# A 1024 x 1024 x 4096 feed-forward product by seven block products in place of eight, and the two feed-forward products one after the other

## The chip, the cores and the metric

The kernel runs on one core of one Trainium2 chip. The metric is the device time of one execution in microseconds: before the change 1409.34 us, the median of three runs (1408.54 to 1409.73). TensorE multiplies matrices and writes PSUM; VectorE, ScalarE and GpSimd do the element-wise work; SyncE issues the DMAs between DRAM and SBUF.

## The reference, cut to what matters

One layer of a hybrid decoder, 1024 tokens, d_model 1024, d_ff 4096, all float32. The change touches only its last lines, and what feeds them:

```
x = x + g1 * (mixed @ w_out[i])
h2 = rms_norm(x, norm2_g[i]) * (1.0 + sc2) + sh2
ff = jnp.square(jax.nn.relu(h2 @ w_ff1[i])) @ w_ff2[i]      # (1024x1024)(1024x4096), then (1024x4096)(4096x1024)
x = x + g2 * ff
```

## The kernel before

Float32 accuracy is made of reduced-precision products. Every operand is split into a high and a low part of type fp32r (`split`, L457: the high part is a rounding copy, the low part a subtraction, L468), and `mm3` (L87 to L91) gives three matmuls for each product: high x high (L89), high x low (L90), low x high (L91). Below, FF1 is `h2 @ w_ff1` with its squared relu, and FF2 the product with `w_ff2`.

`outproj` (L1464) goes over eight blocks of 128 tokens. `proj(t)` is the output projection of a block (48 matmuls into `pS`), then the gated residual and the norm on VectorE (`xn`, L1483 to L1490). `modulate(t)` transposes `xn` on TensorE, scales and shifts it (`h`, L1502 and L1503) and splits it: high parts `h2h` on ScalarE, low parts `h2l` on GpSimd. `h2h` and `h2l` hold the whole of h2, transposed, 128 x 8 x 1024. The products of the first two 128-wide column chunks of `w_ff1` are begun here, in pieces of 512, 384 and 128 tokens, so that the last block's norm is covered.

`ff` (L1535) interleaves the two products. `ff1(c)` computes one of 32 chunks of 128 columns: 48 matmuls of 512 tokens into a pair of PSUM banks (`pS`), relu and square on ScalarE (`ftr`, `ah`), square again and low part on VectorE (`al`, L1590, L1591). The activations never leave SBUF. `ff2(g)` uses two chunks at once: 16 tiles of 128 tokens x 512 columns, six matmuls each, in four rotating banks (`pg`), each added by VectorE into `acc` (L1607, L1609). The weights come by DMA as whole 512 KB chunks (`fraw`) and are split on ScalarE (`w1h`, `w2h`) and GpSimd (`w1l`, `w2l`). FF1 has 32 x 48 = 1536 matmuls of 512 columns, FF2 16 x 96 = 1536. `ada_g2` computes the gate of the last residual on the side, with one-column matmuls (L265).

The tile framework puts the instructions in order on each engine by a simulated timeline; each engine then works strictly in its own order and waits on semaphores.

## Time and profile before

| | us |
|---|---|
| median of three runs | 1409.34 |
| profiled execution | 1406.54 |
| its span | 1404.5 |
| TensorE busy | 1293.0 |
| VectorE busy | 801.2 |
| GpSimd busy | 545.4 |
| ScalarE busy | 516.1 |
| TensorE idle between 684.8 and 1404 us | 4.6 |

The two feed-forward products fill the second half of the span. Busy time of a row is what the profiler attributes to the instructions; for TensorE, matmuls overlap in the pipeline, so their durations are longer than the distance from one start to the next, and the cadence is read from a stretch divided by its count. Of the 4.6 us of idle time (0.54 and 4.07 us in two stretches) the trace puts 1.2 us down to waits for other engines.

### The profile page before, as it was taken

To read this page: it belongs to the slowest core of one execution; us is meant where nothing else is said; L and a number is where in the kernel's file an instruction comes from. 1 tells how busy PE (TensorE), PEld (TensorE's weight loads), DVE (VectorE), ACT (ScalarE), POOL (GpSimd) and SP (SyncE) were. 2 spreads that over 40 slices of the span, in tenths; PEclk is the share of its full clock that TensorE was granted. 3 is DMA by queue.
4 is the path that set the end of the run, shared out by engine and by line. 5 is a ranking of instruction groups with operands and counts; after the bars stand their busy time and mean duration, and the time that the engine had idled before them with its cause. 6 is when DMAs were issued, how large, how long until landed. Compare 5 with 4: busy or idle time off the path is not lost.

```text
span 1404.5 us, 18004 instructions
## 1 busy us (share of the span) xinstructions
PE 1293.0 (92%) x6822; PEld 1107.2 (79%) x6822; DVE 801.2 (57%) x1422; ACT 516.1 (37%) x954; POOL 545.4 (39%) x425
## 2 busy tenths in 40 slices
PE   4978988818898999999999999999999999999998
...
GB/s 334 112 47 39 70 104 124 80 132 25 82 86 98 222 153 87 100 90 108 91 150 105 46 40 36 60 51 55 31 60 60 45 110 72 60 60 45 36 25 119
DMA packets 101656, 121.06 MB, mean 86 GB/s; under 512 B 25408, under 2 KB 75584, under 8 KB 101568
## 3 DMA queue, kind: packets, MB, share of 16 engines
...
q10 hardware_dynamic: 1072, 0.03, 0.0%
...
## 4 chain that ended last, share of the span: by engine, by line
PE 59%; DMA 4%; DVE 2%; ACT 2%; POOL 1%; issue 1%; SPq 0%; ACTq 0%; POOLq 0%; DVEq 0%
PE pS L90 10%; PE pS L89 10%; PE pS L91 10%; PE pg L89 8%; PE pg L91 8%; PE pg L90 8%; DMA awa<-w_ada 3%; PE po L1270 1%; PE pg L265 1%; PE pg L1254 1%; POOL wol L468 1%; DMA woraw<-w_out 1%; ACT P L1243 0%; PE pg L1458 0%; DVE aacc L1401 0%
## 5 line engine op out<-in xcount | busy, mean ns | idle before, releaser
L1609 DVE TENSOR_TENSOR acc<-pg,acc 128x512 f32<-128x512 f32 x240 | 164.5, 689 | 243.0 <-PE pg L91 242.8
L468 POOL TENSOR_TENSOR w2l<-fraw,w2h 128x1024 fp32r<-128x1024 f32 x32 | 78.9, 2488 | 328.4 <-ACT w2h L466 328.4
L90 PE MATMUL pg<-w2l,ah 128*128 128x512 f32 x512 | 201.0, 393 | 0.0
L89 PE MATMUL pg<-w2h,ah 128*128 128x512 f32 x512 | 200.5, 392 | 0.6 <-DVE acc L1607 0.5
L91 PE MATMUL pg<-w2h,al 128*128 128x512 f32 x512 | 200.6, 393 | 0.2 <-DVE al L1591 0.2
L90 PE MATMUL pS<-h2l,w1h 128*128 128x512 f32 (+2 forms) x504 | 198.0, 393 | 0.0
L89 PE MATMUL pS<-h2h,w1h 128*128 128x512 f32 (+2 forms) x504 | 196.9, 391 | 0.0
L91 PE MATMUL pS<-h2h,w1l 128*128 128x512 f32 (+2 forms) x504 | 196.7, 390 | 0.0
L466 ACT ACTIVATE w2h<-fraw 128x1024 fp32r<-128x1024 f32 x32 | 32.2, 1052 | 352.5 <-PE pg L91 352.5
L1590 DVE TENSOR_TENSOR ftr<-ftr 128x1024 f32<-128x1024 f32 x32 | 46.2, 1445 | 129.2 <-ACT ah L1589 129.1
L468 POOL TENSOR_TENSOR w1l<-fraw,w1h 128x1024 fp32r<-128x1024 f32 x30 | 74.1, 2470 | 112.3 <-ACT w1h L466 66.2
L89 PEld LDWEIGHTS pg<-w2h,ah 128*128 128x128 f32 x512 | 96.6, 189 | 23.8 <-DVE acc L1607 1.1
L90 PEld LDWEIGHTS pg<-w2l,ah 128*128 128x128 f32 x512 | 96.6, 189 | 21.9
L91 PEld LDWEIGHTS pg<-w2h,al 128*128 128x128 f32 x512 | 96.3, 188 | 21.8 <-DVE al L1591 0.9
L89 PEld LDWEIGHTS pS<-h2h,w1h 128*128 128x128 f32 x504 | 94.6, 188 | 21.6
L91 PEld LDWEIGHTS pS<-h2h,w1l 128*128 128x128 f32 x504 | 94.6, 188 | 21.0
L90 PEld LDWEIGHTS pS<-h2l,w1h 128*128 128x128 f32 x504 | 94.6, 188 | 20.7
L90 PE MATMUL pg<-wl,hh 128*128 128x256 f32 (+1 forms) x288 | 82.1, 286 | 11.4 <-POOL wl L468 11.4
L466 ACT ACTIVATE w1h<-fraw 128x1024 fp32r<-128x1024 f32 x30 | 31.8, 1060 | 160.9 <-PE pS L90 96.2
L89 PE MATMUL pg<-wh,hh 128*128 128x256 f32 (+1 forms) x288 | 81.4, 286 | 3.6 <-ACT wh L466 2.6
L91 PE MATMUL pg<-wh,hl 128*128 128x256 f32 (+1 forms) x288 | 81.9, 285 | 0.0
L1270 PE MATMUL po<-v,pt 128*128 128x64 f32 x576 | 77.8, 283 | 3.5 <-ACT pt L1257 3.4
...
## 6 DMA issues: line engine op xcount, KB each, us to landing
fraw<-w_ff SPq DMA_DIRECT2D x62, 512.0 KB, 3.8
awa<-w_ada SPq DMA_DIRECT2D x32, 512.0 KB, 4.6
x<-x SPq DMA_DIRECT2D x16, 512.0 KB, 5.1
wa<-w_ada SPq DMA_DIRECT2D x13, 512.0 KB, 7.8
...
x_d<-x SPq DMA_DIRECT2D x8, 512.0 KB, 2.6
```

What stands on the lines that cost most here:

```text
L89: T.matmul(out, lh, rh, start=start, stop=False)
L90: T.matmul(out, lh, rl, start=False, stop=False)
L91: self.pe = T.matmul(out, ll, rh, start=False, stop=stop).ins
L265: nc.tensor.matmul(ps[:, k:k + 1], acc.rearrange("p (q k) -> p k q", k=8)[:, k, :], self.ones[:, 0:1], start=True, stop=True)
L466: nc.scalar.activation(hi, x, AF.Copy)
L468: e.tensor_tensor(lo, x, f(hi), op=OP.subtract)
L1254: T.transpose(ps[:, o:o + 128], P[n][h][:, (k0 + i) * 128:(k0 + i + 1) * 128], self.ident)
L1270: T.matmul(po[:, o:o + HD], pt[:, (2 * i + h) * 128:(2 * i + h + 1) * 128], self.v[:, k0 + i, kv * HD:(kv + 1) * HD], start=(o == 0 and k0 ...
L1590: V.tensor_tensor(tr, tr, tr, op=OP.mult)
L1609: V.tensor_tensor(d, ps, d, op=OP.add)
```

## The change

Each pair of 128-wide chunks of `w_ff1` (16 pairs, 256 columns) is one 2 x 2 block product: blocks of the weights 512 x 128, blocks of h2 512 x 512 (`self.B`: half of the features by half of the tokens). The seven-product form by Winograd is used. With B11 = `b00`, B21 = `b10`, B22 = `b11`, and H0, H1 the two feature halves of the last 512 tokens, T1 = H0 - B11 (made in `modulate`, kept as `b01`), T2 = H1 - T1 (in four score slots, `sx`, tags sc4 to sc7), T3 = T2 - B11 and T4 = B21 - T2 are operands; of the weights four sums are made for each pair (`wsum`). A product is 4 x 3 matmuls, a pair 7 x 12 = 84, where two chunks had 96. PSUM accumulates across products where one is a term of two answers: `keep` copies a bank aside in between, into the slots sc4, sc5 and sc6. `put` adds, applies relu, squares, and the finished activations go to DRAM as float32 (`a_d`, 512 KB twice for each pair). When all pairs are done `ff_down` begins: it loads them back (`araw`), splits them (`ah` on ScalarE, `al` on VectorE), loads and splits `w_ff2` as before, and runs FF2 unchanged. In `split` the sums and the T operands have their low parts on VectorE ("v"), and the sums themselves are made on GpSimd.

```diff
             h2p, h2p_close = self.pool("h2", side="left")
-            self.h2h = h2p.tile([128, KC, L], F32R, name="h2h")
-            self.h2l = h2p.tile([128, KC, L], F32R, name="h2l")
+            self.B = {(kk, hf): [h2p.tile([128, 4, 512], F32R, name=f"b{kk}{hf}{n}") for n in "hl"]
+                      for kk, hf in ((0, 0), (0, 1), (1, 0), (1, 1))}
             self.w1p, w1_close = self.pool("w1", side="left")
-            self.w1first = tuple(self.w1p.tile([128, KC, 128], F32R, name=n) for n in ("w1h", "w1l"))
+            self.gb = gb
             self.outproj(mxp)
             mx_close()
             wop_close()
-            self.ff()
+            self.ff_up()
             w1_close()
+            h2p_close()
+            self.ff_down()
             gb_close()
-            h2p_close()
             scp_close()
...
                 bc = lambda w: w[:, 4 * kk:4 * kk + 4, None].to_broadcast([128, 4, 128])
                 V.tensor_tensor(h, pv, bc(self.s2), op=OP.mult)
                 V.tensor_tensor(h, h, bc(self.b2), op=OP.add)
-                hv = self.h2h[:, 4 * kk:4 * kk + 4, t * 128:(t + 1) * 128]
-                self.split(hv, self.h2l[:, 4 * kk:4 * kk + 4, t * 128:(t + 1) * 128], h, "s", "g")
-
-        def loadw1(c, hi, lo):
+                if hf and kk == 0:
+                    for b in self.B[0, 0]:
+                        V.tensor_tensor(h, h, f(b[:, :, tl]), op=OP.subtract)
+                bh, bl = self.B[kk, hf]
+                self.split(bh[:, :, tl], bl[:, :, tl], h, "s", "g")
+                H.append(h)
+            if hf:
+                self.t2[t - 4] = self.sct(t)
+                V.tensor_tensor(self.t2[t - 4], H[1], H[0], op=OP.subtract)
...
+                self.split(*A[i], raw[:, 4 * i:4 * i + 4], "s", "g")
+
+        self.t2 = {}
...
+            if t >= 5 and t < 7:
+                self.W1[t - 5] = self.w1ab(t - 5)
+                loadw1(2 * (t - 5), self.W1[t - 5])
+        self.ff_ps = {i: self.bank2() for i in range(2)}
+        for i in range(2):
+            self.prod(self.ff_ps[i][:, 0], self.W1[i][0], self.B[0, 0], True)
+            self.prod(self.ff_ps[i][:, 1], self.W1[i][1], self.B[1, 0], True)
+            if i == 0:
                 modulate(NT - 1)
...
+    def sct(self, i, dt=F32, n="sx"):
+
+        t = self.scp.tile([128, max(512, (i + 1) * 128)], dt, name=f"{n}{i}", tag=f"sc{i}")
+        return t[:, :512].rearrange("p (k n) -> p k n", k=4)
+
+    def w1ab(self, i):
+
+        if i % 2:
+            w = [self.sct(j, F32R, "w1x") for j in range(4)]
+        else:
+            w = [self.w1p.tile([128, 4, 128], F32R, name=f"w1a{j}") for j in range(4)]
+        return [w[0:2], w[2:4]]
+
+    def prod(self, o, A, B, start):
+        for k in range(4):
+            self.mm3(o, A[0][:, k], A[1][:, k], B[0][:, k], B[1][:, k], start and k == 0, k == 3, skip_group_check=True)
+
+    def ff_up(self):
+
         nc, a = self.nc, self.a
...
-        fp, fclose = self.pool("ff", side="right")
+        fp, fclose = self.pool("ffu", side="right")
+        NP2 = DFF // 256
+        w1 = a["w_ff1"][0].rearrange("(p k) f -> p k f", k=8)
+        self.a_d = self.dram.tile([DFF // 128, 128, 1024], F32, name="a_d")
+        TT = {n: [fp.tile([128, 4, 512], F32R, name=f"t{n}{x}") for x in "hl"] for n in (2, 3, 4)}
+        B11, T1, B21, B22 = (self.B[q] for q in ((0, 0), (0, 1), (1, 0), (1, 1)))
+        RAW, SUM, W, PS, C = {}, {}, {}, {}, {}
+
+        def load(i):
+            RAW[i] = fp.tile([128, KC, 256], F32, name="w1r", bufs=2)
+            D.dma_start(RAW[i], w1[:, :, i * 256:(i + 1) * 256])
+
+        def quarter(i, r, c):
+            return RAW[i][:, 4 * c:4 * c + 4, r * 128:(r + 1) * 128]
+
+        def wsum(i, n):
+            q = lambda r, c: quarter(i, r, c)
+            x, y, op = {1: lambda: (q(1, 0), q(1, 1), OP.add), 2: lambda: (SUM[i, 1], q(0, 0), OP.subtract),
+                        3: lambda: (q(0, 0), q(1, 0), OP.subtract),
+                        4: lambda: (q(0, 1), SUM[i, 2], OP.subtract)}[n]()
+            SUM[i, n] = fp.tile([128, 4, 128], F32, name="ws", bufs=4)
+            G.tensor_tensor(SUM[i, n], x, y, op=op)
+
+        def form(i, n):
+            if n in ("a", "b"):
+                if i not in self.W1:
+                    self.W1[i] = self.w1ab(i)
+                x, w = quarter(i, 0, "ab".index(n)), self.W1[i]["ab".index(n)]
+            else:
+                x = quarter(i, 1, 1) if n == "d" else SUM[i, n]
+                w = [fp.tile([128, 4, 128], F32R, name="wf", bufs=14) for _ in range(2)]
+            self.split(*w, x, "s", "v")
+            W[i, n] = w
+
+        def tform(n):
+            for t in range(4):
+                tl = slice(128 * t, 128 * t + 128)
+                x = self.t2[t]
+                if n > 2:
+                    x = fp.tile([128, 4, 128], F32, name="ws", bufs=4)
+                    b = [f(z[:, :, tl]) for z in (B11 if n == 3 else B21)]
+                    if n == 3:
+                        G.tensor_tensor(x, self.t2[t], b[0], op=OP.subtract)
+                        G.tensor_tensor(x, x, b[1], op=OP.subtract)
+                    else:
+                        G.tensor_tensor(x, b[0], self.t2[t], op=OP.subtract)
+                        G.tensor_tensor(x, x, b[1], op=OP.add)
+                self.split(TT[n][0][:, :, tl], TT[n][1][:, :, tl], x, "s", "v")
+
+        def half(i, r):
+            if (i, r) not in C:
+                C[i, r] = self.gb.tile([128, 1024], F32, name="c0", tag="g1") if r == 0 else \
+                    self.scp.tile([128, 1024], F32, name="c1", tag="sc7")
+            return C[i, r]
+
+        def put(i, r, c, x, y):
+            o = half(i, r)[:, 512 * c:512 * c + 512]
+            if y is not None:
+                V.tensor_tensor(o, x, y, op=OP.add)
+                x = o
+            else:
+                S.activation(o, x, AF.Relu)
+            V.scalar_tensor_tensor(o, x, 0.0, o, op0=OP.max, op1=OP.mult)
+
+        def keep(i, j, x):
+            o = self.sct(j, n="kp").rearrange("p k n -> p (k n)")
+            S.activation(o, x, AF.Copy)
+            C[i, "k", j] = o
+
+        def step(i, n):
+            if i not in PS:
+                PS[i] = [self.ff_ps[i] if i in self.ff_ps else self.bank2(), None]
+            pa, pb = PS[i][0][:, 0], PS[i][0][:, 1]
+            if n == 1:
+                if i not in self.ff_ps:
+                    self.prod(pa, W[i, "a"], B11, True)
+                keep(i, 4, pa)
+            elif n == 2:
+                if i not in self.ff_ps:
+                    self.prod(pb, W[i, "b"], B21, True)
+                put(i, 0, 0, pb, C.pop((i, "k", 4)))
+            elif n == 5:
+                PS[i][1] = self.bank()
+                self.prod(PS[i][1], W[i, 1], T1, True)
+                keep(i, 6, PS[i][1])
+            elif n == 6:
+                self.prod(pa, W[i, 2], TT[2], False)
+                keep(i, 5, pa)
+            elif n == 7:
+                self.prod(pa, W[i, 3], TT[3], False)
+                put(i, 1, 1, pa, C.pop((i, "k", 6)))
+            elif n == 3:
+                self.prod(PS[i][1], W[i, 4], B22, False)
+                put(i, 0, 1, PS[i][1], C.pop((i, "k", 5)))
+                D.dma_start(self.a_d[2 * i], half(i, 0))
+            elif n == 4:
+                self.prod(pa, W[i, "d"], TT[4], False)
+                put(i, 1, 0, pa, None)
+                D.dma_start(self.a_d[2 * i + 1], half(i, 1))
+
+        ORDER = ((1, "a", ()), (5, 1, (1,)), (6, 2, (2,)), (2, "b", ()), (7, 3, (3,)), (3, 4, (4,)), (4, "d", ()))
+
+        def prep(i, j):
+            if i < NP2:
+                _, w, sums = ORDER[j]
+                for n in sums:
+                    wsum(i, n)
+                form(i, w)
+
+        for i in range(2):
+            load(i)
+        for i in range(2):
+            wsum(i, 1)
+            form(i, 1)
+            wsum(i, 2)
+        tform(2)
+        for i in range(2):
+            form(i, 2)
+        tform(3)
+        for i in range(2):
+            wsum(i, 3)
+            form(i, 3)
+        for i in range(2):
+            wsum(i, 4)
+            form(i, 4)
+        tform(4)
+        for i in range(2):
+            form(i, "d")
+            load(i + 2)
+        for i in range(2):
+            step(i, 1)
+            step(i, 5)
+            step(i, 6)
+            step(i, 2)
+            step(i, 7)
+            step(i, 3)
+            step(i, 4)
+            for j in range(7):
+                if i == 1:
+                    prep(2, j)
+        for i in range(2, NP2):
+            for j, (n, _, _) in enumerate(ORDER):
+                step(i, n)
+                prep(i + 1, j)
+            if i + 2 < NP2:
+                load(i + 2)
+        fclose()
...
+    def ff_down(self):
+        nc, a = self.nc, self.a
+        V, S, G, T, D = nc.vector, nc.scalar, nc.gpsimd, nc.tensor, nc.sync
+        fp, fclose = self.pool("ffd", side="left")
...
+        def loada(c):
+            raw = fp.tile([128, 1024], F32, name="araw", bufs=2)
+            D.dma_start(raw, self.a_d[c])
+            ah = fp.tile([128, 1024], F32R, name="ah", bufs=4)
+            al = fp.tile([128, 1024], F32R, name="al", bufs=4)
+            self.split(ah, al, raw, "s", "v")
             aT[c] = ah, al
+
+        for c in range(GF):
+            load2(c)
+            loada(c)
+        acc = fp.tile([128, NT, 1024], F32, name="acc")
...
         for g in range(n):
-            if g + 1 < n:
-                ff1(2 * g + 2)
-            if g + 2 < n:
-                load1(2 * g + 4)
+            for c in range(2 * g + 2, min(2 * g + 4, NF)):
+                load2(c)
+                loada(c)
             if 0 < g < 7:
                 next(ada, None)
                 next(ada, None)
             if g == 7:
                 D.dma_start(self.g2, self.g_d[1:2, :].to_broadcast([128, 1024]))
             ff2(g, g == n - 1)
-            if g + 1 < n:
-                load2(2 * g + 2)
-                load2(2 * g + 3)
-                ff1(2 * g + 3)
-            if g + 2 < n:
-                load1(2 * g + 5)
         fclose()
```

GpSimd, from the end of the normalisation of the last token block into FF1. Before (`h2l` is the low half of a block, `w1l` and `w2l` low parts of whole weight chunks):

```order
L468 TENSOR_TENSOR h2l<-h_7655,h2h 128x4x128
L468 TENSOR_TENSOR h2l<-h_7665,h2h 128x4x128
L468 TENSOR_TENSOR w1l<-fraw,w1h 128x1024
L468 TENSOR_TENSOR w2l<-fraw,w2h 128x1024 x2
L468 TENSOR_TENSOR w1l<-fraw,w1h 128x1024 x2
L468 TENSOR_TENSOR w2l<-fraw,w2h 128x1024 x2
```

After, the same place (`b01l`, `b11l` are the last block's low halves; L1586 is `wsum`, L1607 and L1608 make T3, L1610 begins T4; two rows like the first and second here stand between them and the last `b01l`):

```order
L1586 TENSOR_TENSOR ws<-w1r 128x512
L1586 TENSOR_TENSOR ws<-ws,w1r 128x512
L1607 TENSOR_TENSOR ws<-sx_7394,b00h 128x512
L1607 TENSOR_TENSOR ws<-sx_7524,b00h 128x512
L1608 TENSOR_TENSOR ws<-ws,b00l 128x512 x2
L1607 TENSOR_TENSOR ws<-sx_7620,b00h 128x512
L1607 TENSOR_TENSOR ws<-sx_7670,b00h 128x512
L1608 TENSOR_TENSOR ws<-ws,b00l 128x512 x2
L1586 TENSOR_TENSOR ws<-w1r 128x512 x2
L1586 TENSOR_TENSOR ws<-w1r,ws 128x512 x2
L1610 TENSOR_TENSOR ws<-b10h,sx_7394 128x512
```

From the last low half on, GpSimd has seventeen operations of 128 x 512 up to the first that reads `sx_7394` for T4, the first of the four T2 slots; before, it had weight splits here.

ScalarE, the same place. Before:

```order
L466 ACTIVATE h2h<-h_7655 128x4x128
L466 ACTIVATE h2h<-h_7665 128x4x128
L466 ACTIVATE w1h<-fraw 128x1024
L1586 ACTIVATE ftr<-pS 128x1024
L466 ACTIVATE w2h<-fraw 128x1024
L1589 ACTIVATE ah<-ftr 128x1024
L466 ACTIVATE w2h<-fraw 128x1024
L1586 ACTIVATE ftr<-pS 128x1024
```

After (`t2h` and `t3h` are high parts of T operands, `wf` of weight operands, `kp` is a copy made by `keep`):

```order
L467 ACTIVATE t2h<-sx_7394 128x4x128
L467 ACTIVATE t2h<-sx_7524 128x4x128
L467 ACTIVATE t2h<-sx_7620 128x4x128
L467 ACTIVATE t2h<-sx_7670 128x4x128
L467 ACTIVATE wf<-ws 128x512 x4
L467 ACTIVATE t3h<-ws 128x4x128 x4
L467 ACTIVATE wf<-ws 128x512 x4
L467 ACTIVATE wf<-w1r 128x512
L1631 ACTIVATE kp_7821<-pS 128x512
L1631 ACTIVATE kp_7836<-pg 128x512
```

The first copy out of a product's bank stands behind four high parts of T3 and the high parts of all eight weight sums of the first two pairs, each of which reads a result of GpSimd.

VectorE, in the middle of FF2. Before (`ftr` and `al` are the square and the low part that FF1's chunks need):

```order
L1609 TENSOR_TENSOR acc<-pg,acc 128x512 x13
L1590 TENSOR_TENSOR ftr<-ftr 128x1024
L1591 TENSOR_TENSOR al<-ftr,ah 128x1024
L1609 TENSOR_TENSOR acc<-pg,acc 128x512 x2
L1590 TENSOR_TENSOR ftr<-ftr 128x1024
L1609 TENSOR_TENSOR acc<-pg,acc 128x512
L1591 TENSOR_TENSOR al<-ftr,ah 128x1024
L1609 TENSOR_TENSOR acc<-pg,acc 128x512 x13
```

After:

```order
L1761 TENSOR_TENSOR acc<-pg,acc 128x512 x15
L469 TENSOR_TENSOR al<-araw,ah 128x1024
L1761 TENSOR_TENSOR acc<-pg,acc 128x512
L469 TENSOR_TENSOR al<-araw,ah 128x1024
L1761 TENSOR_TENSOR acc<-pg,acc 128x512 x15
```

In a group of sixteen accumulations VectorE now has two low parts with one accumulation between them; before it had two squares and two low parts, at two places of the group.

## Rows read from the trace of the kernel before

**Rows 1.** The page: span, busy time by engine, chain by engine.
```profile
span 1404.5 us, 18004 instructions
...
PE 1293.0 (92%) x6822; PEld 1107.2 (79%) x6822; DVE 801.2 (57%) x1422; ACT 516.1 (37%) x954; POOL 545.4 (39%) x425
...
PE 59%; DMA 4%; DVE 2%; ACT 2%; POOL 1%; issue 1%; SPq 0%; ACTq 0%; POOLq 0%; DVEq 0%
```

**Rows 2.** Busy time by stretch; columns: us, each engine's busy us (instructions), clock, DMA.
```profile
684.80:722.00 37.20, 36.66 (x203) 32.17 (x203) 23.23 (x19) 11.51 (x14) 16.85 (x9) 1.00 0.42 132
722.00:1404.00 682.00, 677.93 (x2932) 551.38 (x2930) 281.91 (x339) 119.33 (x118) 178.45 (x72) 1.00 0.19 61
```

**Rows 3.** The same view, TensorE alone, inside the two interleaved products.
```profile
1000.00:1300.00 300.00, 300.00 (x1302) 1.00 0.20 60
```

**Rows 4.** Timeline, TensorE, second product alone: start, us, what; 22 rows from first to last.
```profile
1395.51 0.39 PE L91 MATMUL pg<-w2h,al 128*128 128x512 f32 x1
...
1400.27 0.39 PE L91 MATMUL pg<-w2h,al 128*128 128x512 f32 x1
```

**Rows 5.** What TensorE waited for from 640 us on: us in total, times, longest.
```profile
PE pS L89 <- DVE xn L1483: 0.5, 1, 0.5
PE pg L89 <- DVE acc L1607: 0.5, 1, 0.5
PE pg L91 <- DVE al L1591: 0.2, 1, 0.2
```

**Rows 6.** Timeline, TensorE, end of the last output projection.
```profile
684.61 0.40 PE L91 MATMUL pS<-woh,ml 128*128 128x512 f32 x1
684.85 1.05 PE L1498 MATMUL pg<-ident,xn 128*128 128x128 f32 x8
```

**Rows 7.** Timeline, VectorE, while the last token blocks are normalised.
```profile
642.47 1.21 DVE L1484 TENSOR_TENSOR x<-xn,x 128x1024 f32<-128x1024 f32 x1
643.60 1.79 DVE L1503 TENSOR_TENSOR h<-h,b 128x512 f32<-128x512 f32 x1
...
687.82 0.68 DVE L1503 TENSOR_TENSOR h<-h,b 128x512 f32<-128x512 f32 x1
...
692.14 1.79 DVE L1490 TENSOR_SCALAR xn<-x,ors 128x1024 f32<-128x1024 f32 x1 [0.73 <-POOL ors L85]
```

**Rows 8.** Timeline, GpSimd, the same stretch.
```profile
642.69 2.15 POOL L468 TENSOR_TENSOR h2l<-h,h2h 128x512 fp32r<-128x512 f32 x1 [6.79 <-ACT h2h L466]
...
666.33 2.51 POOL L468 TENSOR_TENSOR w1x<-w1r,w1x 128x512 fp32r<-128x512 f32 x2 [3.26 <-ACT w1x L466]
...
699.19 2.92 POOL L468 TENSOR_TENSOR h2l<-h,h2h 128x512 fp32r<-128x512 f32 x2 [5.81 <-ACT h2h L466]
```

**Rows 9.** Timeline, ScalarE: a copy out of PSUM, a high half.
```profile
640.36 0.58 ACT L1460 ACTIVATE mh<-pg 128x512 fp32r<-128x512 f32 x1
...
673.77 0.63 ACT L466 ACTIVATE h2h<-h 128x512 fp32r<-128x512 f32 x1 [0.47 <-DVE h L1503]
```

**Rows 10.** Timeline, VectorE, a whole tile beside GpSimd's whole tiles.
```profile
711.14 3.31 DVE L1591 TENSOR_TENSOR al<-ftr,ah 128x1024 fp32r<-128x1024 f32 x1
```

**Rows 11.** Timeline, GpSimd, the same stretch.
```profile
707.62 5.74 POOL L468 TENSOR_TENSOR w2l<-fraw,w2h 128x1024 fp32r<-128x1024 f32 x2 [3.18 <-ACT w2h L466]
```

**Rows 12.** Groups of instructions, 690 to 1404 us: line, tiles, count | busy us, mean ns | idle.
```profile
L1609 DVE TENSOR_TENSOR acc<-pg,acc 128x512 f32<-128x512 f32 x240 | 164.5, 689 | 243.0 <-PE pg L91 242.8
...
L468 POOL TENSOR_TENSOR w2l<-fraw,w2h 128x1024 fp32r<-128x1024 f32 x32 | 78.9, 2488 | 328.4 <-ACT w2h L466 328.4
...
L466 ACT ACTIVATE w2h<-fraw 128x1024 fp32r<-128x1024 f32 x32 | 32.2, 1052 | 352.5 <-PE pg L91 352.5
```

**Rows 13.** Timeline, TensorE: the sixteen one-column products of the gate.
```profile
941.10 3.73 PE L265 MATMUL pg<-ones,aacc 128*128 128x1 f32 x16
```

**Rows 14.** Busy time by stretch, TensorE alone, right after them.
```profile
945.66:948.60 2.94, 2.94 (x8) 0.50 0.34 107
```

**Rows 15.** The page, DMA issues: tile, count, KB each, median us to landing.
```profile
fraw<-w_ff SPq DMA_DIRECT2D x62, 512.0 KB, 3.8
```

More of the change, by code (lines that the diff above doesn't have):

```diff
@@ L85, in rstd, with mm3 @@
         nc.gpsimd.tensor_tensor(out, v, self.mhalf[:, :shp[1]], op=OP.pow)
-    def mm3(self, out, lh, ll, rh, rl, start, stop):
+    def mm3(self, out, lh, ll, rh, rl, start, stop, **kw):
         T = self.nc.tensor
-        T.matmul(out, lh, rh, start=start, stop=False)
-        T.matmul(out, lh, rl, start=False, stop=False)
-        self.pe = T.matmul(out, ll, rh, start=False, stop=stop).ins
+        T.matmul(out, lh, rh, start=start, stop=False, **kw)
+        T.matmul(out, lh, rl, start=False, stop=False, **kw)
+        self.pe = T.matmul(out, ll, rh, start=False, stop=stop, **kw).ins
     def build(self):
@@ L1511, in loadw1 @@
             D.dma_start(raw, w1[:, :, c * 128:(c + 1) * 128])
-            n = KC // len(hi)
-            for i, (h, l) in enumerate(zip(hi, lo)):
-                self.split(h, l, raw[:, i * n:(i + 1) * n], "s", "g")
-            return [[w[k // n][:, k % n] for k in range(KC)] for w in (hi, lo)]
-        hi, lo = self.w1first
-        W1 = []
+            for i in range(2):
+                self.split(*A[i], raw[:, 4 * i:4 * i + 4], "s", "g")
+        self.t2 = {}
+        self.W1 = {}
         for t in range(NT):
@@ L1524, in outproj @@
                 modulate(t - 1)
-            if t == 5:
-                W1.append(loadw1(0, [hi], [lo]))
-            if t == 6:
-                w = [self.scp.tile([128, 4, 128], F32R, name=f"w1x{i}", tag=f"sc{i}") for i in range(4)]
-                W1.append(loadw1(1, w[0:2], w[2:4]))
-        P = [self.bank2(), self.bank2()]
-        for a, b in ((0, 512), (512, 896), (896, 1024)):
-            for c in range(2):
-                self.ff1_mm(P[c], *W1[c], a, b)
-            if a == 0:
+            if t >= 5 and t < 7:
+                self.W1[t - 5] = self.w1ab(t - 5)
+                loadw1(2 * (t - 5), self.W1[t - 5])
@@ L1535, in outproj @@
+        self.ff_ps = {i: self.bank2() for i in range(2)}
[3 more added lines that the diff above has]
+            if i == 0:
                 modulate(NT - 1)
-        self.ff_ps = P
         opclose()
-    def ff1_mm(self, ps, hi, lo, a, b):
-        o = ps.rearrange("p j n -> p (j n)")[:, a:b]
-        for k in range(KC):
-            self.mm3(o, hi[k], lo[k], self.h2h[:, k, a:b], self.h2l[:, k, a:b], k == 0, k == KC - 1)
@@ L1545, in ff @@
+    def ff_up(self):
         nc, a = self.nc, self.a
         V, S, G, T, D = nc.vector, nc.scalar, nc.gpsimd, nc.tensor, nc.sync
-        fp, fclose = self.pool("ff", side="right")
+        fp, fclose = self.pool("ffu", side="right")
[115 more added lines that the diff above has]
+            load(i + 2)
+        for i in range(2):
+            step(i, 1)
[15 more added lines that the diff above has]
+        fclose()
@@ L1548, in ff @@
+    def ff_down(self):
+        nc, a = self.nc, self.a
+        V, S, G, T, D = nc.vector, nc.scalar, nc.gpsimd, nc.tensor, nc.sync
+        fp, fclose = self.pool("ffd", side="left")
         NF = DFF // 128
         GF, GC = 2, 9
-        acc = fp.tile([128, NT, 1024], F32, name="acc")
-        w1 = a["w_ff1"][0].rearrange("(p k) f -> p k f", k=8)
         w2 = a["w_ff2"][0].rearrange("(c p) n -> c p n", p=128)
@@ L1621, in ff @@
         n = NF // GF
-        load1(GF)
-        for c in range(GF):
-            load2(c)
-            ff1(c)
-        load1(GF + 1)
         ada = self.ada_g2(fp)
```

32 lines of the change are left out of this document (5 added, 27 removed).

## Prediction

> **What bounds the kernel now.** I read the page first: TensorE is busy for 1293.0 of 1404.5 us and holds 59% of the chain that ended last; DMA, VectorE and ScalarE have 4, 2 and 2% [rows 1]. Then the two feed-forward products by stretches: from 684.80 to 722.00 TensorE is busy for 36.66 of 37.20 us, from 722.00 to 1404.00 for 677.93 of 682.00, at the full granted clock, while VectorE has 281.91, ScalarE 119.33 and GpSimd 178.45 us [rows 2]. So this half of the span is as long as its matmuls. The list of waits confirms it: from 640 us on the interleaved products wait 0.5 us for the last norm, 0.5 us for a copy out of PSUM and 0.2 us for a low part, 1.2 us together [rows 5]. Every matmul taken out pays in full, as long as the others stay fed; that is the question.
>
> **What goes.** 16 x 96 matmuls of FF1 become 16 x 84: 1344 for 1536. In the interleaved stretch 1302 take 300.00 us, 0.2304 us each [rows 3]; 192 fewer are worth 44.2 us. Where FF2 runs alone, 21 steps from 1395.51 to 1400.27 take 4.76 us, 0.2267 each [rows 4]. I take 0.0028 us less for each of FF2's 1536 matmuls, 4.3 us, with 0 and 5.7 (the whole difference) as ends. FF1 keeps 0.2304, because its weights change every matmul as before.
>
> **What comes, beside TensorE.** Prices first. A 128x512 pass over SBUF takes VectorE 0.60 us (half of 1.21 for 1024), GpSimd 1.255 (2.51 for two), ScalarE 0.58 to 0.63 [rows 7 to 9]. VectorE's passes with both inputs in SBUF and GpSimd's passes exclude each other: at 643.60 VectorE's 128x512 takes 1.79 us beside GpSimd, at 687.82 0.68 alone; at 642.69 GpSimd's takes 2.15; of whole tiles VectorE's takes 3.31 and GpSimd's two 5.74 beside it, for 2 x 2.488 in the mean [rows 7, 8, 10 to 12]. Each waits for the other's whole pass, so I add the two engines' times wherever both have work. Passes with PSUM as one input stay at 0.689 us in the mean of 240 [rows 12].
>
> In the steady state of FF1 a pair needs 84 x 0.2304 = 19.4 us of TensorE. GpSimd has four sums, 5.0 us; VectorE seven low parts and three squares, 6.0, and four passes out of PSUM, 2.8; ScalarE seven high parts, three copies, one relu, 6.6. Even added, 13.8 us stay under 19.4: hidden, 0. The extra VectorE work inside the output projection (two subtractions for T1 and one for T2 in each of four blocks, 4 x 1.8 us) lies beside 48 x 0.2267 = 10.9 us of matmuls for each block: 0. The activations add 16 MB written and 16 MB read over some 680 us, 47 GB/s on top of 61 at a DMA share of 0.19; the start of FF1 already ran 132 GB/s at 0.42, and a 512 KB chunk lands in 3.8 us against about 20 us for which a pair or a group lasts [rows 2, 15]: 0.
>
> **The start of FF1.** Before, the last projection matmul starts at 684.61 and the norm is covered with products of the first 512 tokens; 0.5 us is lost [rows 5, 6]. Now the first products of two pairs (48 matmuls) are the only ones that do not need the last block, and everything else needs operands that are made only after it. In steps:
> - the norm ends at 692.14 + 1.79 = 693.9 [rows 7]; transposes 0.5 (half of 1.05 [rows 6]); seven VectorE halves (scale and shift twice, two subtractions, T2) 4.2; two high parts 1.2; two low parts on GpSimd 2.6 and four T2 low parts on VectorE, alternating, 2.4: 704.8.
> - first weight sum 1.26, its high part 0.6: step 5 of the first pair starts at about 706.4. The 48 early products and the transposes end near 694.6 (684.8 + 9.8, as part of them runs before the last projection): idle 11.8. The 24 products of step 5 last 5.5 us, to 712; 1.3 us of waits for the second sum and its low part: 713.1.
> - step 6 adds into the bank that `keep` has to copy first. On ScalarE that copy stands behind T3's high parts and the weight sums; its slot is the one in which T2's first quarter lies, so it also waits for the seventeenth GpSimd pass. 17 x 1.255 = 21.3, and twelve VectorE low parts alternating, 7.2: 704.8 + 28.5 = 733.3, plus 0.6 of copy: 733.9, so idle 20.8. Queued behind this copy on ScalarE are T4's high parts and the next weights.
> - 24 more products, 5.5 us, to 739.4. The copy of step 6 stands behind the second T4 high part, five GpSimd passes (6.3) and six VectorE passes (3.6) later, plus two ScalarE passes: 744.4; idle 5.0.
>
> Together 11.8 + 1.3 + 20.8 + 5.0 = 38.9, less the 0.5 that was there: 38. If VectorE's passes all fell into gaps of GpSimd's queue, 7.2 + 3.6 and the 2.4 would go: 26; if every GpSimd pass took the 2.15 us of the slow row, 22 x 0.9 minus the 10.8 already counted: 47. I take 38, since the rows show the exclusion each time both have work.
>
> The trace shows TensorE's clock falling after it did little: after sixteen one-column products of 3.73 us, eight records from 945.66 on run at a granted 0.50, the 1.2 GHz level [rows 13, 14]: 2.94 us for seven steps that need 1.6, a loss of 1.3. Three long waits here make it likely three times, and more after 20 us: I take +3, with 0 and 6 as ends.
>
> **Between the products.** At the last pair nothing is left to interleave: two answers on VectorE 0.5 + 1.0 past the last product, ScalarE's relu 0.58, two passes of 1.05 (weight and activation) 2.1, GpSimd's weight low part 2.49, and the loads of the first chunks, which stand on the DMA queue behind the write that waits for the answer, 3.8 [rows 9, 12, 15]. Some run side by side: +7, ends 4 and 11.
>
> **FF2 alone.** A group is 96 matmuls, 21.8 us; VectorE has 16 x 0.689 + 2 x 1.21 = 13.4. But its two low parts now stand together, and GpSimd's two weight low parts fall at the same time. In the worst case VectorE is held 2.49 + 1.21 + 0.69 + 2.49 + 1.21 = 8.1 us, while four PSUM banks cover 24 x 0.2276 = 5.5: 2.6 lost, 15 times 39. At the other end is before's 0.7 us of such waits [rows 5], where the low parts stood at two places. I take a quarter of the upper end, 10: the worst case needs all four passes in a row, and an accumulation stands between.
>
> The Trainium skill (Perfetto Trace Analysis, Optimization Strategy) speaks against the change: a kernel with several regimes may gain by interleaving them, and the same gap repeated can mean too few buffers. That the interleaved products wait 1.2 us agrees with it [rows 5]; no run here yet shows them apart. By that rule this term would be the 39; by the row it would be 0.7.
>
> **Sum.** -44.2 - 4.3 + 38 + 3 + 7 + 10 = +9.5 us, against the profiled 1406.54 (span 1404.5 and 2.0 around it): 1416.0. The median of the runs is 2.8 above the profiled one: 1418.8, about 1419. With the start between 34 and 42 and FF2's waits between 5 and 17 the forecast's own range is 1410 to 1430.
>
> **Rivals.**
> 1. The passes do not hold each other up as much, and the groups of FF2 stay fed: -44.2 - 4.3 + 26 + 7 + 1 = -14.5, 1395. It is decided at the start of FF1: if TensorE's idle time there is under 28 us, this holds. For it: GpSimd's mean of 2.488 for a whole tile is hardly above 2 x 1.255, so it is seldom held [rows 8, 12]. Against: VectorE is, and in the start ScalarE's order ties both together.
> 2. As forecast at the start, but FF2 waits no more than before: +9.5 - 10 = -0.5, 1409; with FF2's cadence in FF1 too (1344 x 0.0028 = 3.8) 1405. For it: VectorE's 13.4 of 21.8 us, and before's groups had 16 x 0.689 + 2 x (1.2 + 1.2) = 15.9 without waits.
> 3. FF1's steady state waits: the answers of step 7 must leave the bank before step 4 adds into it, with only step 3's twelve products (2.8 us) between. If VectorE is 2 us late (one GpSimd pass and one of its own) in each of 14 pairs: +28, 1447. For it: a pass of VectorE may wait 1.2 us [rows 7]; against: per pair it has 5 us to spare.
>
> That the products are not saved is none: the order has 84 matmuls for each pair.
>
> **Chances.** Forecast 0.55, first rival 0.17, second 0.18, third 0.10. 0.2% (2.8 us) is about what a measurement of this kernel can tell from no change. Faster: first rival and 0.08 of the second, 0.25. Same: 0.09 of the second and 0.03 of the forecast's low end, 0.12. Slower: the rest, 0.63. The range leaves out the half of the first and most of the third rival: 1396 to 1434.
>
> **What would show it.** Right: 84 matmuls for each pair at about 0.23 us; TensorE idle for some 38 us between the last projection and step 4 of the first pair, in one piece of about 12 and one of about 20, ended by ScalarE's weight copy and by `keep`; GpSimd and VectorE busy in turn there; in FF2 a gap at the end of groups, released by `acc`. Wrong: gaps inside later pairs (third rival), idle under 28 us at the start (first), no gaps in FF2 (second), a long run at the low clock, or loads of `araw` as what TensorE waits for.

## The result and the profile after

The changed kernel takes 1420.93 us (median of six, 1419.14 to 1423.35) beside 1409.16 for the kernel before: 1.008 of it, with a 95% interval of 1.0062 to 1.0097. On a second chip it was 1418.88 beside 1406.14, 1.0095 (1.0074 to 1.0116). It is slower, by 12 to 13 us; 1419 was forecast, inside 1396 to 1434.

First the page of the changed kernel, to be set against [rows 1]:

```profile
span 1418.9 us, 18370 instructions
...
PE 1254.0 (88%) x6582; PEld 1072.4 (76%) x6582; DVE 971.7 (68%) x1634; ACT 560.1 (39%) x1077; POOL 603.3 (43%) x476
...
PE 50%; DVE 10%; DMA 6%; issue 3%; POOL 3%; ACT 2%; SPq 0%; DVEq 0%; POOLq 0%; ACTq 0%
```

The span is 14.4 us longer although TensorE is busy for 39 us less. VectorE's share of the chain went from 2 to 10%, GpSimd's from 1 to 3%. Where this is shows by stretches (columns as in [rows 2]):

```profile
684.80:750.00 65.20, 30.53 (x105) 23.26 (x105) 52.77 (x47) 22.26 (x39) 48.97 (x34) 0.71 0.24 81
750.00:1030.00 280.00, 279.20 (x1213) 227.39 (x1211) 146.83 (x200) 88.73 (x151) 71.42 (x52) 1.00 0.29 101
1030.00:1046.00 16.00, 11.46 (x39) 8.07 (x40) 7.62 (x9) 5.61 (x6) 5.69 (x2) 0.89 0.97 325
1046.00:1418.00 372.00, 353.50 (x1527) 287.86 (x1525) 263.58 (x308) 57.91 (x60) 124.76 (x44) 0.99 0.35 114
```

Inside FF1, from 750 to 1030 us, TensorE is as full as before; at its start it is busy for 30.53 of 65.20 us, at a mean granted clock of 0.71. In the passage to FF2 the DMA engines are at 0.97. What TensorE waited for from 640 us on, as in [rows 5]:

```profile
PE pS L89 <- ACT kp L1631: 15.4, 1, 15.4
PE pg L89 <- DVE acc L1761: 15.3, 10, 3.2
PE pg L89 <- ACT wf L467: 10.3, 1, 10.3
PE pS L89 <- DVE c L1623: 7.2, 3, 6.1
PE pg L89 <- ACT ah L467: 4.1, 2, 2.6
PE pg L91 <- DVE wf L469: 2.0, 1, 2.0
```

The three waits that the prediction named are there: for the first weight sum (`wf`), for the copy `kp`, for the answer that frees the bank of step 7 (`c`). In the timeline of TensorE, from the last projection matmul, which answers to [rows 6]:

```profile
681.95 0.40 PE L91 MATMUL pS<-woh,ml 128*128 128x512 f32 x1
...
691.36 1.15 PE L1501 MATMUL pg<-ident,xn 128*128 128x128 f32 x8 [0.85 <-DVE xn L1491]
702.85 0.80 PE L89 MATMUL pg<-b01h,wf 128*128 128x512 f32 x1 [10.34 <-ACT wf L467]
...
706.08 0.80 PE L91 MATMUL pg<-b01h,wf 128*128 128x512 f32 x1 [2.01 <-DVE wf L469]
706.67 0.63 PE L89 MATMUL pg<-b01h,wf 128*128 128x512 f32 x1
...
729.59 0.80 PE L89 MATMUL pS<-t2h,wf 128*128 128x512 f32 x1 [15.40 <-ACT kp L1631]
...
742.86 0.80 PE L89 MATMUL pS<-t3h,wf 128*128 128x512 f32 x1 [6.08 <-DVE c L1623]
```

681.95 is 2.7 us earlier than before's 684.61. From there the prediction's chain stands 2.7 us earlier too: step 5 was to start at 706.4 - 2.7 = 703.7 and starts at 702.85, step 6 at 731.2 and starts at 729.59, step 7 at 741.7 and starts at 742.86. The rows of 0.63 us, 0.43 from one start to the next, are the low clock behind each wait (granted clock 0.50 from 702.80 to 712.10, the 1.2 GHz level).

### The profile page after: what moved, and what is told of

Same layout as the page of the kernel before. It is cut to its first block, busy times and chain, and to the rows that moved or that the text cites. A ratio compares the mean times of both kernels' runs of the same rounds, so it can differ in the third digit from the quotient of the medians.

```text
span 1418.9 us, 18370 instructions
## 1 busy us (share of the span) xinstructions
PE 1254.0 (88%) x6582; PEld 1072.4 (76%) x6582; DVE 971.7 (68%) x1634; ACT 560.1 (39%) x1077; POOL 603.3 (43%) x476
## 4 chain that ended last, share of the span: by engine, by line
PE 50%; DVE 10%; DMA 6%; issue 3%; POOL 3%; ACT 2%; SPq 0%; DVEq 0%; POOLq 0%; ACTq 0%
PE pg L89 8%; PE pg L90 8%; PE pg L91 8%; PE pS L89 7%; PE pS L90 7%; PE pS L91 7%; DMA awa<-w_ada 3%; PE po L1271 2%; DMA x<-x_d 2%; DVE acc L1761 2%; DVE al L469 1%; PE pg L266 1%; PE pg L1255 1%; DVE acc L1765 1%; POOL ws L1586 1%
## 5 line engine op out<-in xcount | busy, mean ns | idle before, releaser
L89 PE MATMUL pg<-w2h,ah 128*128 128x512 f32 x512 | 202.9, 397 | 19.7 <-DVE acc L1761 15.3
L467 ACT ACTIVATE ah<-araw 128x1024 fp32r<-128x1024 f32 x32 | 33.7, 1054 | 274.4 <-PE pg L90 235.6
L91 PEld LDWEIGHTS pg<-w2h,al 128*128 128x128 f32 x512 | 97.2, 190 | 20.4
L469 DVE TENSOR_TENSOR wf<-ws,wf 128x512 fp32r<-128x512 f32 x64 | 68.6, 1075 | 57.3 <-PE pS L90 45.9
L1586 POOL TENSOR_TENSOR ws<-w1r 128x512 f32<-128x512 f32 x32 | 47.1, 1471 | 95.3 <-DMA w1r<-w_ff 81.3
L1271 PEld LDWEIGHTS po<-v,pt 128*128 128x128 f32 x576 | 76.5, 205 | 6.2 <-ACT pt L1258 3.8
L467 ACT ACTIVATE wf<-ws 128x512 fp32r<-128x512 f32 x64 | 40.3, 632 | 99.2 <-PE pg L90 40.9
L557 DVE SCALAR_TENSOR_TENSOR sc<-r,wsgn,sc 128x384 f32<-128x384 f32 (+5 forms) x42 | 57.5, 1381 | 26.9 <-ACT r L553 25.8
L469 DVE TENSOR_TENSOR al<-araw,ah 128x1024 fp32r<-128x1024 f32 x32 | 64.4, 2012 | 5.2 <-ACT ah L467 5.2
L90 PEld LDWEIGHTS pg<-wl,hh 128*128 128x128 f32 x288 | 55.3, 192 | 12.5 <-POOL wl L469 11.9
L89 PEld LDWEIGHTS pg<-wh,hh 128*128 128x128 f32 x288 | 54.7, 192 | 5.0 <-ACT wh L467 2.8
L1242 DVE CUSTOM_DVE_ANT_0 P<-pS,sc,rq 128x384 f32<-128x384 f32 (+5 forms) x48 | 44.0, 942 | 20.0 <-PE pS L1238 12.8
```

What stands on the lines that cost most here:

```text
L89: T.matmul(out, lh, rh, start=start, stop=False, **kw)
L90: T.matmul(out, lh, rl, start=False, stop=False, **kw)
L91: self.pe = T.matmul(out, ll, rh, start=False, stop=stop, **kw).ins
L467: nc.scalar.activation(hi, x, AF.Copy)
L469: e.tensor_tensor(lo, x, f(hi), op=OP.subtract)
L557: V.scalar_tensor_tensor(sc, rv, self.wsgn[:, qt, h:h + 1], sc, op0=OP.mult, op1=OP.add)
```

## Experiments

Each kernel differs from the changed one in what its diff shows (the first from the kernel before), and ran beside the kernel before on the same chip; the ratio is to that. One distance is compared throughout: from the start of the last projection matmul to the first matmul of FF2 ("FF1's stretch", 353.99 us in the changed kernel, 354.31 on the second chip), and from there to the last matmul of FF2 ("FF2's stretch", 378.63 and 377.31).

> The changed kernel itself beside the next three, so that they stand against it on one chip: 1.008 of the kernel before (1.006 to 1.010), TensorE idle for about 34.7 us at the start of FF1, 15.3 us of waits for acc in FF2.

Measured 1.0095 (1.0074 to 1.0116): as before, with 34.8 us of idle time at the start and 14.0 of waits for `acc`.

**The sequence alone.**

```diff
             self.outproj(mxp)
...
-            self.ff()
+            self.ff_up()
             w1_close()
+            h2p_close()
+            self.ff_down()
...
+            tr = fp.tile([128, 1024], F32, name="ftr", bufs=2)
+            S.activation(tr, ps.rearrange("p j n -> p (j n)"), AF.Relu)
+            V.tensor_tensor(tr, tr, tr, op=OP.mult)
+            D.dma_start(self.a_d[c], tr)
```

> Only the sequence, without the seven-product form: FF1 has its eight block products (1536 matmuls of 512 columns) as in the kernel before, but all of FF1 runs first, the squared activations go through DRAM, and FF2 follows exactly as in the changed kernel. Theory (the start of FF1 eats the saved matmuls, the sequence costs extra on top): no long wait at the start of FF1 (under 3 us), some 7 us at the passage between the products and some 15 us of waits for acc in FF2, against 4.3 us of better cadence: about 1427 us (1422 to 1433), slower than both kernels. Rival (the sequence is free, everything is lost in the start of FF1): 1405 to 1410 us.

Measured 1433.93 us, 1.0198 (1.0179 to 1.0217). The direction is the theory's, but 28 us over the kernel before where it had 18. The waits of TensorE:

```profile
PE pg L89 <- DVE acc L1630: 16.0, 13, 3.2
PE pg L89 <- ACT ah L467: 6.2, 1, 6.2
...
PE pg L89 <- DVE acc L1628: 1.5, 2, 1.3
PE pS L89 <- DVE xn L1484: 0.5, 1, 0.5
```

No wait at the start of FF1 but 0.5 us; 17.5 for `acc` and 6.2 at the passage. So the sequence by itself costs 28 us, and the seven-product form gives back 14 to 17 (1.0198 less 1.008 to 1.0095, of 1405), where 44 were saved: FF1's stretch falls from 365.71 to 354 us only. Of the 10 us that I missed, 3 are the cadence (1.2 of the 4.3 came, see below) and 2.5 the waits for `acc`; much of the rest is in slower steps of TensorE beside the waits, which I had not counted: 52 steps from start to start last over 0.28 us with no wait in them, 17 in the kernel before, and they cost 5.6 us more.

**All sums on VectorE.**

```diff
-            G.tensor_tensor(SUM[i, n], x, y, op=op)
+            V.tensor_tensor(SUM[i, n], x, y, op=op)
...
-                        G.tensor_tensor(x, self.t2[t], b[0], op=OP.subtract)
-                        G.tensor_tensor(x, x, b[1], op=OP.subtract)
+                        V.tensor_tensor(x, self.t2[t], b[0], op=OP.subtract)
+                        V.tensor_tensor(x, x, b[1], op=OP.subtract)
```

> The changed kernel with all sums of weights and of T3 and T4 on VectorE in place of GpSimd. Theory (at the start of FF1 the two engines exclude each other, so that their passes add, 1.255 and 0.6 us each): 17 x 0.6 + 12 x 0.6 = 17.4 us in place of 28.5 for the wait at step 6; idle TensorE time at the start falls from 34.7 to about 23, the time by about 12 us to 1409 (1405 to 1413). Rival (the engines work side by side, and VectorE with 29 passes on one queue becomes the longer one): idle time at the start the same or longer, 1419 to 1426.

Measured 1404.06 us, 0.9996 (0.9976 to 1.0015), 12 to 14 us under the changed kernel. In the changed kernel GpSimd's timeline has, from the first sum to the first operation of T4:

```profile
700.43 1.70 POOL L1586 TENSOR_TENSOR ws<-w1r 128x512 f32<-128x512 f32 x1
...
707.13 3.40 POOL L1607 TENSOR_TENSOR ws<-sx,b00h 128x512 f32<-128x512 f32 x2
...
714.09 1.26 POOL L1607 TENSOR_TENSOR ws<-sx,b00h 128x512 f32<-128x512 f32 x1 [0.63 <-DVE t3l L469]
...
727.19 5.09 POOL L1610 TENSOR_TENSOR ws<-b10h,sx 128x512 f32<-128x512 f32 x3
```

The seventeenth operation is the first of the three at 727.19; with 5.09/3 = 1.70 us it ends at 728.9, and `kp` starts at 728.94. 728.9 - 700.4 = 28.5 us for the seventeen, the prediction's 28.5. The passes last 1.70 us where VectorE has work, 1.26 where they wait for it. With the sums on VectorE its own timeline has:

```profile
704.52 0.68 DVE L1586 TENSOR_TENSOR ws<-w1r 128x512 f32<-128x512 f32 x1
...
721.03 0.68 DVE L1610 TENSOR_TENSOR ws<-b10h,sx 128x512 f32<-128x512 f32 x1
```

From 704.52 to the end of the same operation at 721.6 it is 17.1 us (17.4 expected), and TensorE's wait for `kp` is 8.1 us in place of 15.4; idle at the start is 20.4 us, with about 23 expected. FF1's stretch is 339.20 us, 15 less. The theory holds, the rival is out; that the engines exclude each other is not yet shown by it, since GpSimd's passes are also slower ones.

**More tiles for the sums.** In the changed kernel's rows some of GpSimd's passes wait 0.63 us for a tile, so four tiles could have been the cause of the turn-taking.

```diff
-            SUM[i, n] = fp.tile([128, 4, 128], F32, name="ws", bufs=4)
+            SUM[i, n] = fp.tile([128, 4, 128], F32, name="ws", bufs=7)
...
-                    x = fp.tile([128, 4, 128], F32, name="ws", bufs=4)
+                    x = fp.tile([128, 4, 128], F32, name="ws", bufs=7)
```

> The changed kernel with seven tiles for the sums (ws) in place of four. In the changed kernel's trace GpSimd waits 0.63 us before several of its passes for a low part of VectorE that frees a tile of ws. Theory (the two engines exclude each other while both have work, whoever has a tile free): the 0.63 us waits turn into longer passes, the seventeen passes still take 27 to 29 us from the first sum to the copy before step 6, time within 3 us of the changed kernel (1.007 to 1.011 of the kernel before). Rival (four tiles are too few, and that alone makes the engines take turns): 17 x 1.255 = 21.3 us, some 7 us less at the start, 1.003 to 1.005.

Measured 1424.76 us, 1.0122 (1.0087 to 1.0157): no gain, and FF1's stretch is 354.2 us, as in the changed kernel. The middle lies just outside the theory's band, on the side away from the rival; what is more lies in FF2's stretch (383.4 us), where the edit changes nothing, and is not explained. GpSimd, then VectorE:

```profile
698.19 1.71 POOL L1586 TENSOR_TENSOR ws<-w1r 128x512 f32<-128x512 f32 x1
...
711.19 1.28 POOL L1586 TENSOR_TENSOR ws<-w1r 128x512 f32<-128x512 f32 x1
712.43 6.27 POOL L1608 TENSOR_TENSOR ws<-ws,b00l 128x512 f32<-128x512 f32 x4
...
723.68 6.32 POOL L1610 TENSOR_TENSOR ws<-b10h,sx 128x512 f32<-128x512 f32 x4
```

```profile
713.17 1.07 DVE L469 TENSOR_TENSOR wf<-ws,wf 128x512 fp32r<-128x512 f32 x1 [4.32 <-ACT wf L467]
```

The waits are gone. Of the seventeen passes fourteen last 1.60 to 1.73 us; the other three, the one at 711.19 among them, last 1.26 to 1.29, and they start in the 4.32 us in which VectorE is idle. The seventeenth ends at 725.4, 27.2 us from the first sum, with 21.3 expected by the rival. So it is not the tiles: the engines hold each other up. The Trainium skill (SBUF — State Buffer, Who interferes with whom) says that a VectorE instruction with two SBUF inputs contends with a GpSimd instruction that reads SBUF; these rows agree. But a GpSimd pass grows by 0.3 to 0.5 us, less than the 0.60 of a whole VectorE pass.

**The copies of `keep` elsewhere.**

```diff
-            o = self.sct(j, n="kp").rearrange("p k n -> p (k n)")
+            o = fp.tile([128, 512], F32, name=f"kp{j}")
...
-                w = [fp.tile([128, 4, 128], F32R, name="wf", bufs=14) for _ in range(2)]
+                w = [fp.tile([128, 4, 128], F32R, name="wf", bufs=11) for _ in range(2)]
```

> The changed kernel with the copies of keep in tiles of their own in place of the score slots sc4, sc5 and sc6, in which T2's quarters lie; to make room the pool of weight parts has 11 tiles in place of 14. Theory (the chain of element-wise passes that makes T3, T4 and the sums sets the end of the start, the slot only where its wait shows): the wait before step 6 breaks up and comes back later, idle time at the start 31 to 38 us, time within 3 us of the changed kernel (1418 to 1424). Rival (the shared slot is the cause of the 15.4 us wait): that wait goes and nothing takes its place, idle time at the start about 20, 1406 to 1411.

Measured 1417.87 us, 1.0089 (1.0065 to 1.0113): the time of the theory. Its idle time is not: 28.0 us at the start (0.9, 10.3, 2.0, 2.0, 2.2, 0.6, 6.6 and 3.4), less than the 31 I had.

```profile
PE pg L89 <- ACT wf L467: 10.3, 1, 10.3
PE pg L89 <- ACT kp L1631: 6.6, 1, 6.6
PE pS L89 <- DVE c L1623: 4.5, 3, 3.4
...
PE pS L89 <- ACT kp L1631: 2.0, 1, 2.0
```

The 15.4 us wait broke into several: with the slot free, step 6 starts 28.4 us after the last projection in place of 47.6, and the waits come behind it. Still 6.7 us less idle made FF1's stretch only 1.7 to 2.0 us shorter (352.33). Between 690 and 770 us 44 matmuls run at the low clock, 28 in the changed kernel: 16 x 0.2 = 3.2 us of what was won went into slow matmuls. That the three tiles fewer for weight parts cost something was not tried apart; in the trace no weight pass of ScalarE waits for TensorE to free a tile before 754 us.

**The waits filled.** So what does the clock cost?

```diff
+        def warm(n, after):
+            with self.tc.issue_after(after):
+                ps = self.bank()
+                for j in range(n):
+                    m = T.matmul(ps, self.W1[0][0][0][:, j % 4], B11[0][:, j % 4], start=True, stop=True, skip_group_check=True).ins
+            return m
...
+                m = warm(40, self.tr)
+                with self.tc.issue_after(m):
+                    step(i, 5)
+                m = warm(60, self.pe)
+                with self.tc.issue_after(m):
+                    step(i, 6)
```

> The changed kernel with 100 matmuls of 512 columns added whose result nobody reads: 40 behind the last transposes, where TensorE waits 10.3 us for step 5, and 60 before step 6, where it waits 15.4. Theory (27 matmuls behind the three long waits run at the 1.2 GHz level, 0.427 us each in place of 0.2276, because TensorE had done nothing before them): kept busy, it stays at the full granted clock, and the 27 x 0.2 = 5.4 us come back, though 23 us of work are added: 0.9965 of the changed kernel, some 4 to 6 us less. Rival (the low clock has nothing to do with the waits, or the added matmuls delay what follows): the same time or up to 10 us more.

Measured 1420.54 us, 1.0112 (1.0092 to 1.0132), beside 1.0095: the rival's result. The clock did as the theory says, the time did not. First the stretch from 680 to 770 us of the changed kernel, then of this one (us, TensorE busy and count, granted clock, DMA):

```profile
680.00:770.00 90.00, 55.33 (x217) 0.79 0.24 82
```

```profile
680.00:770.00 90.00, 78.83 (x325) 0.94 0.25 82
```

The clock's mean goes from 0.79 to 0.94, slow matmuls from 28 to 16; FF1's stretch is 352.25 us, 1.7 to 2.1 shorter, not 5.4. Behind the slow matmuls of step 5 stands the next wait, whose end GpSimd and ScalarE set: step 6 starts 48.0 us after the last projection, in the changed kernel 47.6, so a quicker step 5 only waits longer. That only slow matmuls behind the last wait count is my reading; it was not tried apart.

**FF2 without GpSimd.**

```diff
-                G.tensor_tensor(raw, raw, self.g2, op=OP.mult)
+                V.tensor_tensor(raw, raw, self.g2, op=OP.mult)
...
-            self.split(hi, lo, raw, "s", "g")
+            self.split(hi, lo, raw, "s", "v")
             W2[c] = hi, lo
```

> The changed kernel with GpSimd taken out of FF2: the low parts of w_ff2 and the products with g2 on VectorE. Theory (the waits for acc in FF2 come from VectorE's low parts being held by GpSimd's weight low parts, 8.1 us at a time against 5.5 that four banks cover): VectorE has 4 x 1.21 + 16 x 0.69 = 15.9 us in a group of 21.8, never held, 4.8 us of low parts in a row; waits for acc fall from 15.3 to 3 to 6 us, the time by about 10 us to 1411 (1408 to 1415). Rival (VectorE is late because it has too much to do in the sequence, whoever holds it): its work grows by 2.4 to 4.8 us a group, waits for acc grow, 1421 to 1435.

Measured 1409.65 us, 1.0033 (1.0019 to 1.0047): 7 to 9 us under the changed kernel, FF2's stretch 368.0 us, 9 to 11 shorter (the kernels with the changed kernel's FF2 have 375.8 to 383.4). The waits for `acc`, changed kernel above 15.3 us in 10, at most 3.2:

```profile
PE pg L89 <- DVE acc L1761: 6.5, 8, 1.3
```

6.5 us, a little over the 3 to 6 expected, though VectorE does more in each group. How the 15.3 came about, in one group of the changed kernel: GpSimd, VectorE, and TensorE's two waits.

```profile
1087.62 5.72 POOL L469 TENSOR_TENSOR w2l<-fraw,w2h 128x1024 fp32r<-128x1024 f32 x2 [18.20 <-ACT w2h L467]
```

```profile
1083.31 1.28 DVE L1402 SCALAR_TENSOR_TENSOR aacc<-awa,silc,aacc 128x1024 f32<-128x1024 f32 x1 [1.61 <-DMA awa<-w_ada]
...
1088.26 2.85 DVE L1402 SCALAR_TENSOR_TENSOR aacc<-awa,silc,aacc 128x1024 f32<-128x1024 f32 x1 [1.86 <-DMA awa<-w_ada]
1091.04 0.68 DVE L1761 TENSOR_TENSOR acc<-pg,acc 128x512 f32<-128x512 f32 x1
1091.63 2.79 DVE L469 TENSOR_TENSOR al<-araw,ah 128x1024 fp32r<-128x1024 f32 x1
...
1094.95 1.21 DVE L469 TENSOR_TENSOR al<-araw,ah 128x1024 fp32r<-128x1024 f32 x1
```

```profile
1091.77 0.50 PE L89 MATMUL pg<-w2h,ah 128*128 128x512 f32 x1 [1.28 <-DVE acc L1761]
...
1095.08 0.50 PE L89 MATMUL pg<-w2h,ah 128*128 128x512 f32 x1 [1.64 <-DVE acc L1761]
```

While GpSimd makes two low parts (5.72 us), VectorE's pass of 1.28 us takes 2.85 and the first low part 2.79, where the second, alone, takes 1.21; the accumulations stand behind them, and TensorE waits 1.28 and 1.64 us for a bank.

**Combined.** Sums on VectorE, FF2 without GpSimd, copies of `keep` in their own tiles; the same with 36 unread matmuls; and the first two edits alone (diffs as above).

> Three of the edits at once: all sums on VectorE, the copies of keep in tiles of their own (11 tiles for weight parts), FF2 without GpSimd. Theory (the terms are separate places and add; with VectorE twice as quick in the sums, the slot of keep is now what ends the wait before step 6, so that it pays here though it did not alone): 12 us at the start, some 6 more from the slot, 6.6 in FF2: about 25 us under the changed kernel, 0.990 of the kernel before (0.986 to 0.994). Rival (they overlap: VectorE becomes the bound once all is on it): 10 to 15 us under the changed kernel, 0.998 to 1.001 of the kernel before.

> The combined kernel with 36 unread matmuls behind the last transposes, where TensorE waits about 10 us for step 5. Theory: the clock stays up at the first products of step 5, some 10 steps at 0.2 us, 2 us less than the combined kernel. Rival: no difference, since the shorter waits that follow set the clock back anyway.

> The combined kernel without the tiles of their own for keep: sums on VectorE, FF2 without GpSimd, slots and pools else as in the changed kernel. Theory (as the two traces with sums on VectorE have the same distance from the last projection to FF2, 339.2 and 338.8 us, the slot of keep costs nothing): as the combined kernel, 0.9945 of the kernel before (0.992 to 0.997). Rival (the slot costs the 6 us that I had put down for it): 0.998 to 1.000.

Measured 1396.32 us, 0.9945 (0.9926 to 0.9964); 1397.45, 0.9949 (0.9931 to 0.9967); 1400.68, 0.9948 (0.9928 to 0.9968). All three beat the kernel before; the first was to have 0.990. The two edits add up: FF1's stretch is 338.8, 338.5 and 338.6 us, 15 less, FF2's 369.05 in the first, 8 to 10 less. The 6 us that I put down for the slot are not there, nor the 2 us for the filled wait. Without the slot the wait before step 6 is 2.0 us, but another stands where T4's high part is late:

```profile
PE pg L89 <- ACT wf L467: 11.0, 1, 11.0
PE pS L89 <- ACT t4h L467: 7.3, 1, 7.3
PE pg L89 <- DVE acc L1761: 6.7, 8, 1.3
...
PE pS L89 <- ACT kp L1631: 2.0, 1, 2.0
```

## Why the prediction was right, point by point

The terms against the profiled executions (1406.54 before, 1420.67 after; spans 1404.5 and 1418.9):

| term | forecast | measured |
|---|---|---|
| matmuls saved (189 x 0.2304) | -44.2 | -43.5 |
| cadence (FF1 0.2300, FF2 0.2267) | -4.3 | -6.2 |
| start of FF1, idle | +38 | +34.1 |
| passage, idle | +7 | +5.2 |
| FF2, waits for `acc` | +10 | +14.6 |
| low clock, restarts and the rest | +3 | +12.8 |
| ahead of the last projection | 0 | -2.7 |

The measured column adds to +14.3, of 14.4 between the spans. The medians moved by 11.8, 2.6 us less than the spans, and no term is known better than that. That the forecast came within 2 us is luck in part: errors of up to 10 us cancel, and the 2.8 us that it added between profiled execution and median were those of the kernel before; after the change they are 0.3. The last term is no step of the change: among the changed kernel and its variants the last projection starts anywhere from 679.1 to 687.1 us. The last but one is what remains of the stretch from the last projection to the last matmul (732.62 us in place of 715.66) when the others are taken off.

- **Matmuls saved.** Behind the last projection there are 2863 for 3052, 189 fewer, since 17 of FF1's stood ahead of it for 20. Right.
- **Cadence.** The number came out, 6.2 us for 4.3, but the reason did not hold. I divided the interleaved stretch by its count, 0.2304, gave FF2 the 0.2267 of [rows 4] and let FF1 keep the mean, since its weights change every matmul. FF2's do too: the page counts a weight load for every matmul (PE and PEld x6582). And the mean is of two: in the timeline of TensorE before, 36 steps that are all FF1's lie between these two rows:

```profile
799.66 0.39 PE L91 MATMUL pS<-h2h,w1l 128*128 128x512 f32 x1
...
808.06 0.39 PE L91 MATMUL pS<-h2h,w1l 128*128 128x512 f32 x1
```

These are 8.40 us apart, 0.2333 a step. With eight products in sequence FF1 keeps that, and what FF2 gains by running alone FF1 loses: (1516 x 0.2333 + 1536 x 0.2267) / 3052 is 0.2300, hardly under the mean. The seven-product FF1 runs faster. TensorE alone, first in FF1 of the sequence with eight products, then in FF1 and FF2 of the changed kernel (us, busy us and count, granted clock, DMA; a count takes in one or two matmuls that reach in from before):

```profile
720.00:1040.00 320.00, 320.00 (x1373) 1.00 0.28 89
```

```profile
750.00:1020.00 270.00, 270.00 (x1176) 1.00 0.30 102
1320.00:1380.00 60.00, 60.00 (x266) 1.00 0.22 71
```

From first to last start that is 0.2333, 0.2300 and 0.2267 us a step, and against the mean 1327 x 0.0004 + 1536 x 0.0037 = 6.2 us. Without the step from 0.2333 to 0.2300, which nobody forecast, 4.4 us of it would be missing.
- **The start of FF1.** Mechanism right in each piece: idle 0.85 + 10.34 + 2.01 + 15.40 + 6.08 = 34.7, less 0.54. Seventeen passes in 28.5 us as worked out, though made up otherwise: above 17 x 1.255 there are 3.4 us of longer passes and 3.8 us of waits for tiles (one sum was off by 0.3: 704.8 + 1.26 + 0.6 is 706.7, not 706.4). What the prediction had named beside it, that `keep` also waits for T2's slot, is so and sets where the wait stands: with tiles of its own step 6 starts 19 us earlier. But it costs little: FF1's stretch is 1.7 to 2.0 us shorter with the sums on GpSimd, no shorter with them on VectorE. What holds the start is the chain of passes behind it.
- **Clock.** This term was the most mis-sized: 12.8 us for the 3 that I took, with 6 as the upper end. From the last projection on, 43 steps last 0.38 to 0.45 us where before 8 did, which is 7 us, and 20 of them lie in the passage and in FF2; most of the rest are single slower steps beside the waits. More slow steps after the longest wait did not come: twelve of 0.43 us stand behind the waits of 10.34 and 2.01 us, five behind that of 15.40. As a price it is wrong the other way: the 28 slow matmuls at the start are 5.6 us, but keeping TensorE busy there gives back 2 at most.
- **Passage.** 0.32 + 0.78 + 2.58 + 1.56 = 5.2 us. The last of these is a wait for the second chunk of activations. Its load, issued at 1035.12 behind the write of the last answer, is there at 1041.07, 5.9 us later, while the DMA engines are busy for 0.97 of the time: I had counted 3.8 us for it, not that the first loads share the engines.
- **FF2.** That GpSimd's low parts hold VectorE up is shown by the kernel without GpSimd there. But the picture of the two low parts as enough for it was right only in part. The 15.3 us are ten waits, and nine of them stand in groups in which VectorE also has the gate's passes (L1402), the product with g2 (L1765) or the last residual (L1769), which I had put at nothing; the one in a group with the low parts alone is 1.7 us. So a quarter of the upper end came near for another reason.
- **The rivals.** The first needed under 28 us of idle time at the start: 34.7. The second needed no waits for `acc`: 15.3. The third needed waits in later pairs: from 750 to 1030 us TensorE is busy for 279.20 of 280.00. The Trainium skill's rule on interleaving (Perfetto Trace Analysis, Optimization Strategy) points the right way, since the sequence alone costs 28 us; of gaps that repeat it has 17.5, not 39.

Of the 28 us that the sequence with eight products costs, 23 are waits (24.2 us, before's 1.2) and some 8 slower steps beside them and at the low clock; 1 comes back by the cadence, and its last projection lies 2 us earlier. What stays open is why three streams of matmuls of one size follow each other at 0.2333, 0.2300 and 0.2267 us.
